# A two-layer hybrid decoder on one core: the same instructions with their SBUF buffers at other addresses

## The chip, the cores and the metric

The kernel runs on one core of one Trainium2 chip. The metric is device microseconds (us) for one execution of the whole program. Its engines are TensorE (PE for the matmuls, PEld for the loads of their weights), VectorE (DVE), ScalarE (ACT), GpSimd (POOL) and SyncE (SP), which issues the transfers from memory.

## The reference

Two layers act on x of 256 x 1024 float32. Cut to what matters here:

```
h = rms_norm(x, g_mix);  z = h @ w_in                 # 1024 -> 6072 columns
o_a, o_b, o_c = mla(z...), conv31(z...), nsa(z...)    # three mixers, each -> 1024
x = x + (g_a*o_a + g_b*o_b + g_c*o_c) @ w_out         # g = sigmoid of 3072 of z's columns
h = rms_norm(x, g_ffn)
x = x + square(relu(h @ w_ff1)) @ w_ff2               # 1024 -> 4096 -> 1024
```

## The kernel before

The large products are made in float32 precision from pieces that TensorE takes at full rate: each operand is split into a rounded high part and the remainder, hi + lo, and each product is three matmuls (hi·hi, hi·lo, lo·hi) into one PSUM bank. `piece` (lines 141 to 155) brings 128 x 1024 floats of a weight matrix into `raw` by one transfer, ACT rounds them into `hi` (line 153) and DVE writes the rest into `lo` (line 154).

There are two forms of product:

- `gemm_b` (lines 159 to 165) is channel-major. The weights are the stationary operand (128 columns, loaded anew for each matmul), and the activations stream past as 256 columns. The input projection (tile `psB` of `take`), the mixers' own projections (`wo` of `w_o`) and the first feed-forward product (`ff1`, shown as `ff`) have this form. A piece feeds 24 matmuls: 8 blocks k (or two times 4 in `w_o`), three each. Over both layers that are 1776 matmuls for `psB`, 576 for `wo`, and 1536 for `ff`.
- `gemm_a` (lines 167 to 173) is token-major. The activations are stationary, and the weights stream past as 512 columns. The second feed-forward product (`f0` to `f3`, shown as `f`, 768 matmuls), the product with w_out (its tiles are named `wo0` to `wo3` and show as `wo` too, but with 512 columns and tile `mh`, 192 matmuls) and the first projections (`psA`, 192 with 512 columns and 96 with 312) have it.

In the feed-forward stage one group is two `ff1` pieces (48 matmuls of 256 columns) and then four weight halves of the second product (24 matmuls of 512 columns), 16 groups a layer. Order of work: a priority for each step is written by hand (TRACE, URGENCY); the order of each engine's instructions is fixed when the program is built.

Where buffers lie is set by the tile pools. A pool places its tags one behind another, and a tag's buffers (`bufs`) lie one row length apart, so a row length that is no multiple of 256 bytes moves each next buffer to another place modulo 256. `hi` and `lo` have four buffers each of 1040 floats (4160 bytes, 16 x 256 + 64), taken in rotation. The table has the start of each buffer in the built program, modulo 256 bytes.

| buffer | role | before | after |
|---|---|---|---|
| hh, hl, oh, ol, h2, l2, mh, ml (tags hh, hl) | activations; stream in `gemm_b`, stationary in `gemm_a` | 128 | 64 |
| hi, lo, four buffers each | weights; stationary in `gemm_b`, stream in `gemm_a` | 128, 192, 0, 64 | 128 |
| hi2, lo2 (tag big, shown as hi, lo too) | weights that stream in `psA`, `wo` and `f` | 192 | 64 |
| rh, rl (tag pa, six buffers) | activations of the second feed-forward product, stationary | 192, 0, 64, 128, 192, 0 | 64 |
| yh, yl (tags cv, s2) | activations of `wo` for the convolution | 224 or 192, 128 | 64, 64 |
| raw | weights as transferred | 128 | 128 |

Blocks within a buffer lie a multiple of 256 bytes apart (512 for a block of weights, 1024 for a block of activations), so they leave these places as they are. Below, the offset of a matmul is the place of the stationary operand that is loaded next less that of the operand that streams meanwhile, modulo 256. In `gemm_b` before, the offsets are 0, 64, 128 and 192, one for each buffer of `hi` and `lo`.

Of the kernel before, what the change touches and what calls it, by code (L numbers as in the profile page):

```python
# [8 lines left out]
F32 = mybir.dt.float32  # L9
R32 = mybir.dt.float32r  # L10
# [3 lines left out]
ALU = mybir.AluOpType  # L14
AX = mybir.AxisListType

P = 128
D = 1024
T = 256
# [66 lines left out]
def trunk_kernel(ctx: ExitStack, tc: tile.TileContext, A, out, depth=DEPTH):  # L86
# [3 lines left out]
    wp = ctx.enter_context(tc.tile_pool(name="wp", bufs=3))  # L90
    ap_ = ctx.enter_context(tc.tile_pool(name="ap", bufs=1))
    sp = ctx.enter_context(tc.tile_pool(name="sp", bufs=2))
# [5 lines left out]
    def stat(n, name, dt=F32):  # L98
        return sp.tile([P, n], dt, tag="st%d" % n, name=name, bufs=2 if n > 64 else 6)

    S2 = 6
    PA = 6
    RB = 5
    S1 = 5
    WB = 4
# [5 lines left out]
    stt = nc.vector.scalar_tensor_tensor  # L111
# [24 lines left out]
    def raw(src, n):  # L136
        r = wp.tile([P, 1024], F32, tag="raw", name="raw", bufs=RB)[:, :n]
        nc.sync.dma_start(out=r, in_=src)
        return r

    def piece(src, k, ring=0, half=0):

        n = src.shape[-1]
        r = raw(src, n)
        if ring == 0:
            hi = wp.tile([P, 1040], R32, tag="hi", name="hi", bufs=WB)[:, :n]
            lo = wp.tile([P, 1040], R32, tag="lo", name="lo", bufs=WB)[:, :n]
        else:
            if half == 0:
                ring2[0] = (ap_.tile([P, 2048], R32, tag="big", name="hi2", bufs=BIG),  # L150
                            ap_.tile([P, 2048], R32, tag="big", name="lo2", bufs=BIG))
            hi, lo = (t[:, half * 1024:half * 1024 + n] for t in ring2[0])
        act(hi, r, AF.Copy)  # L153
        tt(out=lo, in0=r, in1=hi.bitcast(F32), op=ALU.subtract)  # L154
        return tuple(t.rearrange("p (k n) -> p k n", k=k) for t in (hi, lo))
# [23 lines left out]
    def rsqrt(v, p, n, name):  # L179

        s = stat(n, name + "_s", I32)
        y = stat(n, name + "_y")
        h = stat(n, name + "_h")
        t = stat(n, name + "_t")
        s, y, h, t = s[:p], y[:p], h[:p], t[:p]
        ts(out=s, in0=v.bitcast(I32), scalar1=1, scalar2=None, op0=ALU.logical_shift_right)
        ts(out=h, in0=v, scalar1=-0.5, scalar2=None, op0=ALU.mult)
        ts(out=y.bitcast(I32), in0=s, scalar1=-1, scalar2=0x5f3759df, op0=ALU.mult, op1=ALU.add)
        for _ in range(3):
            if n == 1:  # L190
                ts(out=t, in0=y, scalar1=y, scalar2=h, op0=ALU.mult, op1=ALU.mult)
                ts(out=y, in0=t, scalar1=1.5, scalar2=y, op0=ALU.add, op1=ALU.mult)
            else:
                tt(out=t, in0=y, in1=y, op=ALU.mult)
                tt(out=t, in0=t, in1=h, op=ALU.mult)
                stt(out=y, in0=t, scalar=1.5, in1=y, op0=ALU.add, op1=ALU.mult)
        return y
# [11 lines left out]
                op0=ALU.mult, op1=ALU.subtract)  # L209

    scaled = [None]
    splits = [None, None]
    tail_priority = [0]

# [11 lines left out]

    def sumsq_row(b, name, v):

        q = sp.tile([P, D // 2], F32, tag="s2", bufs=S2, name=name + "_q")
        s = stat(2, name + "_ss")  # L230
        for i in range(2):
            act(q, x[:, b, i * 512:(i + 1) * 512], AF.Square, accum_out=s[:, i:i + 1])
        tt(out=v, in0=s[:, 0:1], in1=s[:, 1:2], op=ALU.add)
        ts(out=v, in0=v, scalar1=1.0 / D, scalar2=EPS, op0=ALU.mult, op1=ALU.add)
        return v
# [18 lines left out]
    def layer(l):  # L254
# [15 lines left out]
        def s1(name):  # L270
            return sp.tile([P, T], F32, tag="s1", bufs=S1, name=name)

        def pa(name, dt=F32):
            return sp.tile([P, 528], dt, tag="pa", bufs=PA, name=name)[:, :512]

        hB = lambda t: (lambda k: t[k] if isinstance(t, list) else t[:, k, :])
        hA = lambda t, b: (lambda k: t[:, k, b * P:(b + 1) * P])
        col = lambda ap: ap.rearrange("p (n o) -> p n o", o=1)


        hh = ap_.tile([P, 8, T], R32, tag="hh", name="hh", bufs=2)
        hl = ap_.tile([P, 8, T], R32, tag="hl", name="hl", bufs=2)
        grow = raw(bass.AP(tensor=A["gmix"].tensor, offset=A["gmix"].offset + l * D, ap=[[0, P], [1, D]]), D)
        vs = stat(2, "n1v")
        for b in range(NB):
            now = tc.cur_priority
            if l > 0 and b == 0:

                tc.cur_priority = tail_priority[0]
            normed(x[:, b], b, rsqrt(sumsq_row(b, "n1", vs[:, b:b + 1]), P, 1, "n1"), grow, hh, hl, "n1t")  # L290
            if b == 0:
                behind = (scaled[0], splits[0], splits[1])
            tc.cur_priority = now
# [27 lines left out]
        def part_a(i):  # L321

            return ([psum(t, "psA%d" % i) for t in (("at", "at"), ("po", "ch"), ("at", "at"))[i]],
                    [piece(A["wA%d" % i][l, kp], 2, ring=int(i == 1), half=kp % 2) for kp in range(4)])

        def add_a(i, pw, b, kps=range(4)):
            for kp in kps:
                wh, wl = pw[1][kp]
                gemm_a(pw[0][b][:, :A_COLS[i]], hA(hh, b), hA(hl, b), lambda k: wh[:, k, :], lambda k: wl[:, k, :],
                       [(k, kp * 2 + k) for k in range(2)], first=(kp == 0), last=(kp == 3))  # L330


        def take(*names):

            ps = psum("mm", "psB")
            res = []
            for m, nm in enumerate(names):
                wh, wl = piece(A["wB"][l, B_TILES.index(nm)], 8)
                o = ps[:, m * T:(m + 1) * T]
                gemm_b(o, lambda k: wh[:, k, :], lambda k: wl[:, k, :], hB(hh), hB(hl), [(k, k) for k in range(8)])  # L340
                res.append((nm, o))
            return res, ps


        kr = ap_.tile([P, NB, 32], F32, tag="kr", name="kr")
        sg = ap_.tile([P, NB, 24], F32, tag="sg", name="sg")
        vsw = ap_.tile([P, NB, 2, P], F32, tag="vsw", name="vsw")
# [42 lines left out]
        def a_queries():  # L390
            nonlocal nr
            pw = part_a(2)
            psA = pw[0]
            for kp in range(4):
                for b in range(NB):
                    add_a(2, pw, b, (kp,))
            if l == 0:
                sp.tile([P, 8], F32, tag="gap2", name="gap2", bufs=1)
            for b in range(NB):
                pq = psA[b].rearrange("p (g j d) -> p g j d", g=2, j=4)  # L400
                sq = pa("nsqq").rearrange("p (n d) -> p n d", d=DH)
                qn.append(pa("qn").rearrange("p (n d) -> p n d", d=DH))
                act(sq.rearrange("p (j g) d -> p g j d", g=2), pq, AF.Square)
                act(qn[b].rearrange("p (j g) d -> p g j d", g=2), pq, AF.Copy)
                nc.vector.tensor_reduce(out=nst[:, b, 0:8], in_=sq, axis=AX.X, op=ALU.add)
            nv = stat(24, "nv")
            ts(out=nv, in0=nst.rearrange("p b n -> p (b n)"), scalar1=1.0 / DH, scalar2=EPS, op0=ALU.mult, op1=ALU.add)
            nr = rsqrt(nv, P, 24, "nr").rearrange("p (b n) -> p b n", b=NB)
# [330 lines left out]
                heads_T(xk, i, b, kTm, K("vk"), True)  # L739


        upad = sp.tile([P, 4, T + 30], F32, tag="cv", name="upad", bufs=2)
        ca = sp.tile([P, 4, T], F32, tag="cv", name="ca", bufs=2)

        def glu(i):
            if i == 0:
                nc.gpsimd.memset(upad[:, :, 0:30], 0.0)
            res, _ = take(("ua", i), ("ug", i))
            a_, g_ = s1("ua"), s1("ug")
            act(a_, res[0][1], AF.Identity, scale=0.5, bias=hv[:, i:i + 1])  # L750
            act(g_, res[1][1], AF.Tanh, scale=0.5, bias=hv[:, 4 + i:5 + i])  # L751
            stt(out=upad[:, i, 30:], in0=g_, scalar=1.0, in1=a_, op0=ALU.add, op1=ALU.mult)

        def taps(k0, k1):
            for k in range(k0, k1):
# [51 lines left out]
        def w_o(wn, th_, tl_, ko, c2):  # L807
            wh, wl = piece(A[wn][l, c2], 4)
            ps = psum("mm", "wo")
            for u in range(2):  # L810
                gemm_b(ps[:, u * T:(u + 1) * T], lambda k: wh[:, k, u * P:(u + 1) * P],
                       lambda k: wl[:, k, u * P:(u + 1) * P], hB(th_), hB(tl_), [(k, k + ko) for k in range(4)])
            return ps
# [85 lines left out]
        for b in range(NB):  # L899
            v = sumsq_row(b, "n2", stat(1, "n2_v"))  # L900
            rv = stat(1, "rv")
            nc.vector.reciprocal(rv, v)
            r2.append(rv)
# [23 lines left out]
    for l in range(depth):  # L927
        layer(l)
# [129 lines left out]
```

## Time and profile before

| | |
|---|---|
| three timed runs | 923.03, 923.93 and 928.15 us, median 923.93 |
| the profiled execution | 923.36 us, of which its instructions span 921.3 us |
| PE busy | 899.2 us, 98% of the span |
| DVE, ACT, POOL busy | 642.1, 537.3, 27.1 us |
| read from memory | 149.45 MB, 163 GB/s over the span |

[...] The duration does not tell how fast they follow each other; the difference between the starts of two matmuls, divided by the number of steps between them, does. It is called the pace below. The timeline shows starts to 10 ns, so over a run of 24 (23 steps) a pace is known to about half a nanosecond.

### The profile page before, as it was taken

To read this page: it belongs to the slowest core of one execution; us is meant where nothing else is said; L and a number is where in the kernel's file an instruction comes from. 1 tells how busy PE (TensorE), PEld (TensorE's weight loads), DVE (VectorE), ACT (ScalarE), POOL (GpSimd) and SP (SyncE) were. 2 spreads that over 40 slices of the span, in tenths; PEclk is the share of its full clock that TensorE was granted. 3 is DMA by queue.
4 is the path that set the end of the run, shared out by engine and by line. 5 is a ranking of instruction groups with operands and counts; after the bars stand their busy time and mean duration, and the time that the engine had idled before them with its cause. 6 is when DMAs were issued, how large, how long until landed. Compare 5 with 4: busy or idle time off the path is not lost.

```text
span 921.3 us, 16102 instructions
## 1 busy us (share of the span) xinstructions
PE 899.2 (98%) x6214; PEld 796.1 (86%) x6214; DVE 642.1 (70%) x1431; ACT 537.3 (58%) x987; POOL 27.1 (3%) x80
## 2 busy tenths in 40 slices
PE   5999999999999999999999999999999999999998
PEld 4899887699988999999878989877999889999996
DVE  6599988865787565555576989979558785555552
ACT  5456576987466554444355575779865575444430
POOL 3210000000000000000001000000000000000000
PEclk9999999999999999999999999999999999999999
DMA  8644622344556665665345563225436476555621
GB/s 286 219 164 147 218 87 80 115 134 140 181 188 204 210 203 185 190 194 186 102 160 188 165 217 104 79 80 183 155 97 199 151 262 211 185 191 193 188 92 46
DMA packets 43133, 151.55 MB, mean 164 GB/s; under 512 B 4784, under 2 KB 5680, under 8 KB 43056
## 3 DMA queue, kind: packets, MB, share of 16 engines
q1 hardware_dynamic: 43056, 150.52, 49.7%
q8 instruction: 49, 0.80, 0.4%
q14 instruction: 28, 0.23, 0.1%
HBM read 149.45 MB, written 1.05 MB: 163 GB/s over the span
## 4 chain that ended last, share of the span: by engine, by line
PE 89%; DVE 5%; DMA 3%; ACT 3%; issue 1%; SPq 0%; DVEq 0%; ACTq 0%
PE psB L163 7%; PE psB L165 7%; PE psB L164 7%; PE f L173 6%; PE f L171 6%; PE f L172 6%; PE ff L163 6%; PE ff L164 6%; PE ff L165 6%; PE wo L163 3%; PE wo L164 3%; PE wo L165 2%; DVE lo L154 2%; PE nS L578 2%; PE psA L172 2%; PE psA L173 2%
## 5 line engine op out<-in xcount | busy, mean ns | idle before, releaser
L154 DVE TENSOR_TENSOR lo<-raw,hi 128x1024 fp32r<-128x1024 f32 (+1 forms) x266 | 317.7, 1209 | 170.6 <-ACT hi L153 135.8
L153 ACT ACTIVATE hi<-raw 128x1024 fp32r<-128x1024 f32 (+1 forms) x266 | 274.2, 1048 | 256.1 <-DMA raw<-in_ff_dram 108.4
L163 PE MATMUL psB<-hh,hi 128*128 128x256 f32 x592 | 171.4, 290 | 1.5 <-ACT ug L751 1.4
L165 PE MATMUL psB<-hh,lo 128*128 128x256 f32 x592 | 169.1, 287 | 0.0
L164 PE MATMUL psB<-hl,hi 128*128 128x256 f32 x592 | 168.4, 285 | 0.0
L163 PE MATMUL ff<-h,hi 128*128 128x256 f32 x512 | 143.2, 281 | 0.0
L165 PE MATMUL ff<-h,lo 128*128 128x256 f32 x512 | 143.1, 280 | 0.0
L164 PE MATMUL ff<-l,hi 128*128 128x256 f32 x512 | 143.0, 280 | 0.0
L163 PEld LDWEIGHTS psB<-hh,hi 128*128 128x128 f32 x592 | 111.8, 189 | 8.3 <-issue 4.4
L165 PEld LDWEIGHTS psB<-hh,lo 128*128 128x128 f32 x592 | 111.5, 189 | 3.0 <-issue 2.6
L164 PEld LDWEIGHTS psB<-hl,hi 128*128 128x128 f32 x592 | 111.8, 189 | 0.3
L760 DVE SCALAR_TENSOR_TENSOR ca<-upad,cols,ca 128x256 f32<-128x256 f32 x240 | 103.7, 478 | 0.3
L173 PE MATMUL f<-hi,rl 128*128 128x512 f32 x256 | 101.1, 395 | 1.4 <-DVE rl L894 1.4
L171 PE MATMUL f<-hi,rh 128*128 128x512 f32 x256 | 100.9, 394 | 1.2 <-ACT rh L892 1.1
L172 PE MATMUL f<-lo,rh 128*128 128x512 f32 x256 | 100.6, 393 | 0.0
L163 PEld LDWEIGHTS ff<-h,hi 128*128 128x128 f32 x512 | 96.7, 189 | 1.2
L164 PEld LDWEIGHTS ff<-l,hi 128*128 128x128 f32 x512 | 96.5, 189 | 1.3
L165 PEld LDWEIGHTS ff<-h,lo 128*128 128x128 f32 x512 | 96.5, 189 | 0.0
L173 PEld LDWEIGHTS f<-hi,rl 128*128 128x128 f32 x256 | 48.0, 188 | 13.6 <-DVE rl L894 2.6
L171 PEld LDWEIGHTS f<-hi,rh 128*128 128x128 f32 x256 | 48.2, 188 | 11.2 <-ACT rh L892 1.6
L172 PEld LDWEIGHTS f<-lo,rh 128*128 128x128 f32 x256 | 48.1, 188 | 9.9
L172 PE MATMUL psA<-lo,hh 128*128 128x512 f32 (+1 forms) x96 | 36.4, 379 | 1.3 <-DVE lo L154 1.3
(279 smaller groups left out, 1420.2 us busy)
## 6 DMA issues: line engine op xcount, KB each, us to landing
raw<-in_ff_dram SPq DMA_DIRECT2D x128, 512.0 KB, 4.1
raw<-in_wB_dram SPq DMA_DIRECT2D x74, 512.0 KB, 4.0
raw<-in_wA_dram SPq DMA_DIRECT2D x16, 512.0 KB, 4.4
raw<-in_w_out_dram SPq DMA_DIRECT2D x16, 512.0 KB, 3.4
raw<-in_wo_nsa_dram SPq DMA_DIRECT2D x8, 512.0 KB, 4.9
raw<-in_wo_mla_dram SPq DMA_DIRECT2D x8, 512.0 KB, 3.8
raw<-in_wconv_dram SPq DMA_DIRECT2D x8, 512.0 KB, 3.5
raw<-in_wA_dram SPq DMA_DIRECT2D x8, 312.0 KB, 5.2
```

Source lines behind the costliest of these rows:

```text
L153: act(hi, r, AF.Copy)
L154: tt(out=lo, in0=r, in1=hi.bitcast(F32), op=ALU.subtract)
L163: mm(ps, lhsT=wh(kw), rhs=ah(ka), start=(first and i == 0), stop=False)
L164: mm(ps, lhsT=wh(kw), rhs=al(ka), start=False, stop=False)
L165: mm(ps, lhsT=wl(kw), rhs=ah(ka), start=False, stop=(last and i == n - 1))
L171: mm(ps, lhsT=ah(ka), rhs=wh(kw), start=(first and i == 0), stop=False)
L172: mm(ps, lhsT=ah(ka), rhs=wl(kw), start=False, stop=False)
L173: mm(ps, lhsT=al(ka), rhs=wh(kw), start=False, stop=(last and i == n - 1))
L578: mm(pS[g].rearrange("p (h z k) -> p h z k", h=nj, z=2)[:, i], lhsT=qTn[gs, 2 * jp + j, b * P:(b + 1) * P], rhs=kTn[gs, :, 0:nk], start=Tr ...
L760: stt(out=ca[:, i], in0=upad[:, i, k:k + T], scalar=K("wdw", 31 * i + k), in1=ca[:, i], op0=ALU.mult, op1=ALU.add)
```

## The change

The change alters row lengths and adds tiles that nothing uses (`gap0`, `gap1`, `gap3`, `gap4`, and a longer `gap2`). `hi` and `lo` get rows of 1024 floats instead of 1040, the tag `pa` 512 instead of 528, and the convolution's padded input 288 columns instead of 286, of which the last two are not used. No instruction is added, removed or moved: on each engine the built program has the same operations on the same tiles in the same order before and after, apart from the numbers of buffers and lines. Only addresses differ, as in the table: in all `gemm_b` products the offset becomes 64, and in the second feed-forward product the streaming and the stationary operand are at the same place (offset 0), except for its last group in each layer, whose weights are in `hi` and `lo` and stream at offset 192.

```diff
-            hi = wp.tile([P, 1040], R32, tag="hi", name="hi", bufs=WB)[:, :n]
-            lo = wp.tile([P, 1040], R32, tag="lo", name="lo", bufs=WB)[:, :n]
+            hi = wp.tile([P, 1024], R32, tag="hi", name="hi", bufs=WB)[:, :n]
+            lo = wp.tile([P, 1024], R32, tag="lo", name="lo", bufs=WB)[:, :n]
...
+        if name == "n1" and not gapped:
+            gapped.append(sp.tile([P, 16], F32, tag="gap4", name="gap4", bufs=1))
...
-            return sp.tile([P, 528], dt, tag="pa", bufs=PA, name=name)[:, :512]
+            return sp.tile([P, 512], dt, tag="pa", bufs=PA, name=name)
...
+        if l == 0:
+            ap_.tile([P, 48], F32, tag="gap0", name="gap0")
         hh = ap_.tile([P, 8, T], R32, tag="hh", name="hh", bufs=2)
...
+        if l == 0:
+            ap_.tile([P, 48], F32, tag="gap1", name="gap1")
         kr = ap_.tile([P, NB, 32], F32, tag="kr", name="kr")
...
-                sp.tile([P, 8], F32, tag="gap2", name="gap2", bufs=1)
+                sp.tile([P, 64], F32, tag="gap2", name="gap2", bufs=1)
...
-        upad = sp.tile([P, 4, T + 30], F32, tag="cv", name="upad", bufs=2)
+        if l == 0:
+            sp.tile([P, 40], F32, tag="gap3", name="gap3", bufs=1)
+        upad = sp.tile([P, 4, T + 32], F32, tag="cv", name="upad", bufs=2)
```

## Rows read from the trace of the kernel before

**Rows 1.** The page's part 1 and 2: engines and the granted clock

```profile
PE 899.2 (98%) x6214; PEld 796.1 (86%) x6214; DVE 642.1 (70%) x1431; ACT 537.3 (58%) x987; POOL 27.1 (3%) x80
...
PEclk9999999999999999999999999999999999999999
```

**Rows 2.** The page's part 4: the chain that ended last, by engine

```profile
PE 89%; DVE 5%; DMA 3%; ACT 3%; issue 1%; SPq 0%; DVEq 0%; ACTq 0%
```

**Rows 3.** The page's part 5: matmul groups, count, busy us, mean ns

```profile
L163 PE MATMUL psB<-hh,hi 128*128 128x256 f32 x592 | 171.4, 290 | 1.5 <-ACT ug L751 1.4
L163 PE MATMUL ff<-h,hi 128*128 128x256 f32 x512 | 143.2, 281 | 0.0
L173 PE MATMUL f<-hi,rl 128*128 128x512 f32 x256 | 101.1, 395 | 1.4 <-DVE rl L894 1.4
```

**Rows 4.** Timeline of PE, first feed-forward product: start us, us, line, tiles

```profile
336.69 0.28 PE L163 MATMUL ff<-h,hi 128*128 128x256 f32 x1
...
339.30 0.28 PE L165 MATMUL ff<-h,lo 128*128 128x256 f32 x1
...
347.90 0.28 PE L163 MATMUL ff<-h,hi 128*128 128x256 f32 x1
...
350.63 0.28 PE L165 MATMUL ff<-h,lo 128*128 128x256 f32 x1
350.75 0.28 PE L163 MATMUL ff<-h,hi 128*128 128x256 f32 x1
...
353.46 0.28 PE L165 MATMUL ff<-h,lo 128*128 128x256 f32 x1
...
361.85 0.28 PE L163 MATMUL ff<-h,hi 128*128 128x256 f32 x1
...
364.61 0.28 PE L165 MATMUL ff<-h,lo 128*128 128x256 f32 x1
...
443.15 0.28 PE L163 MATMUL ff<-h,hi 128*128 128x256 f32 x1
...
445.86 0.28 PE L165 MATMUL ff<-h,lo 128*128 128x256 f32 x1
```

**Rows 5.** Timeline of PE, products psB: one run of 24

```profile
206.82 0.28 PE L163 MATMUL psB<-hh,hi 128*128 128x256 f32 x1
...
209.53 0.28 PE L165 MATMUL psB<-hh,lo 128*128 128x256 f32 x1
```

**Rows 6.** Timeline of PE, second feed-forward product: where three stretches begin or end

```profile
331.16 0.39 PE L171 MATMUL f<-hi,rh 128*128 128x512 f32 x1
...
342.29 0.40 PE L171 MATMUL f<-hi,rh 128*128 128x512 f32 x1
...
353.58 0.39 PE L171 MATMUL f<-hi,rh 128*128 128x512 f32 x1
...
359.12 0.28 PE L163 MATMUL ff<-h,hi 128*128 128x256 f32 x1
```

**Rows 7.** Timeline of PE, 512-column products psA and wo

```profile
43.20 0.39 PE L173 MATMUL psA<-hi,hl 128*128 128x512 f32 x1
...
45.49 0.28 PE L163 MATMUL psB<-hh,hi 128*128 128x256 f32 x1
...
713.99 0.40 PE L171 MATMUL wo<-hi,mh 128*128 128x512 f32 x1
...
715.38 0.39 PE L171 MATMUL wo<-hi,mh 128*128 128x512 f32 x1
```

**Rows 8.** Windows: us, busy us and instructions of PE, PEld, DVE, ACT, POOL

```profile
60.00:90.00 30.00, 29.27 (x238) 27.71 (x237) 29.93 (x65) 19.62 (x41) 0.00 (x0) 1.00 0.47 150
...
285.00:470.00 185.00, 183.11 (x1173) 165.10 (x1173) 107.80 (x129) 89.84 (x119) 0.00 (x0) 1.00 0.57 181
```

**Rows 9.** The page's part 5: the splitting group of DVE

```profile
L154 DVE TENSOR_TENSOR lo<-raw,hi 128x1024 fp32r<-128x1024 f32 (+1 forms) x266 | 317.7, 1209 | 170.6 <-ACT hi L153 135.8
```

More of the change, by code (lines that the diff above doesn't have):

```diff
@@ L211, in trunk_kernel @@
     scaled = [None]
+    gapped = []
     splits = [None, None]
@@ L751, in glu @@
             act(g_, res[1][1], AF.Tanh, scale=0.5, bias=hv[:, 4 + i:5 + i])
-            stt(out=upad[:, i, 30:], in0=g_, scalar=1.0, in1=a_, op0=ALU.add, op1=ALU.mult)
+            stt(out=upad[:, i, 30:T + 30], in0=g_, scalar=1.0, in1=a_, op0=ALU.add, op1=ALU.mult)
         def taps(k0, k1):
```

## The prediction

> **What bounds the kernel now.** I read the page from the top. [...] The groups of part 5 then show what PE does: `psB`, `ff` and `f`, nearly without idle time before them [rows 3]. So the time is the number of matmuls times the pace at which they follow each other, and the group's mean durations (281, 290 and 395 ns) can't tell that pace, because matmuls overlap. I took it from the timeline, as the distance of starts.
>
> In the first feed-forward product each of the four weight buffers has a pace of its own [rows 4]. The runs of 24 (23 steps) take, by offset:
>
> - offset 0: 364.61 - 361.85 = 2.76 us, 120.0 ns a matmul;
> - offset 128: 350.63 - 347.90 = 2.73 us, 118.7 ns;
> - offset 192: 353.46 - 350.75 = 2.71 us, 117.8 ns;
> - offset 64: 339.30 - 336.69 = 2.61 us, 113.5 ns, but 445.86 - 443.15 = 2.71 us, 117.8 ns, in another run.
>
> [...] Offset 64 has two paces, and a run that is at one keeps it for all its 24 matmuls. Of the 15 unbroken runs of 24 at offset 64 in this product (the first is at 314.21, the last at 897.71 us; two stand in [rows 4]) 11 have the fast pace and 4 the slow one, a mean of 114.6 ns. The instructions and tiles are the same in all of these runs; the buffer is what differs. Pace and place go together in `psB` too, where one run at offset 64 takes 209.53 - 206.82 = 2.71 us, the slow pace [rows 5]; there some two fifths of the matmuls at offset 64 have the fast pace, since small products break its runs and each new start settles anew: a mean of 0.4 x 113.5 + 0.6 x 117.8 = 116.1 ns.
>
> **The change part by part.** All instructions stay, so each term is a number of matmuls by a difference of paces.
>
> First feed-forward product, 1536 matmuls [rows 3]: the four offsets hold a quarter each, (120.0 + 118.7 + 117.8 + 114.6) / 4 = 117.8 ns. After, all are at offset 64, 114.6 ns if the two paces share the runs as now. 3.2 ns x 1536 = 4.9 us less.
>
> `psB`, 1776 matmuls [rows 3], of which some 1460 follow their neighbour without a break: (120.0 + 118.7 + 117.8 + 116.1) / 4 = 118.2 now, 116.1 after, 2.1 x 1460 = 3.1 us less.
>
> `wo` of the mixers, 576 matmuls, three quarters of the way of `ff`, as their runs are mostly unbroken: 3.0 x 560 = 1.7 us less.
>
> `f`, 768 matmuls of 512 columns. Three stretches of 24 take 336.69 - 331.16 = 5.53, 347.90 - 342.29 = 5.61 and 359.12 - 353.58 = 5.54 us [rows 4, 6], which is 230.4, 233.8 and 230.8 ns, a mean of 231.7. They go to offset 0, where no matmul of `f` lies with both neighbours now. The nearest rows are six in a row of the w_out product at offset 0: 715.38 - 713.99 = 1.39 us, 231.7 ns [rows 7]. That is the mean of today, so I take the row and a change of 0.0; the best pace of any 512-column run here is that of ten `psA` matmuls at offset 192, 45.49 - 43.20 = 2.29 us, 229.0 ns [rows 7], and the worst the middle stretch above. The bounds are 2.1 us less and 1.6 us more. I put 0.4 us on the slow side, because in the 256-column product offset 0 is the slowest place.
>
> The other PE work (`psA`, w_out, transposes, attention) also gets new places: `psA` and w_out lose an offset of 192 in part and get one of 0 in part, between 229.0 and 231.7 ns on 384 matmuls, at most 1.0 us either way; I take 0.
>
> DVE and ACT: their operands move too. The 258 full splits of DVE have a mean of 1.22 us in each of the four buffers, with no more than 3 ns between them (their group is [rows 9]), so I cost their new places at nothing. What they hide behind is PE; between 60 and 90 us, DVE is busy for 29.93 of 30 us [rows 8], and the same stretch of the second layer is like it. There PE can't win: some 430 `psB` matmuls by 2.1 ns are 0.9 us that I give back. In the feed-forward stage DVE has 107.80 of 185 us and ACT 89.84 [rows 8], which is room enough for a PE that is 3% faster.
>
> Sum: -4.9 - 3.1 - 1.7 + 0.4 + 0.9 = -8.4 us. The profiled execution took 923.36 us, of which 2.1 lie around the span; it comes to 915.0. That execution is 0.6 us under the median of the timed runs, 923.93; I predict **915.3 us**.
>
> [...]
>
> **The rivals.**
>
> All runs settle at the fast pace. For it: nothing between the pieces changes the offset any more, and a run keeps its pace; after `f`, five of the six starts at offset 64 in the first layer went to the fast one (the run at 336.69 [rows 4] is one). Against it: in `psB` the breaks stay. The price: 4.3 x 1536 + 4.7 x 1460 + 4.3 x 560 = 15.9 us, less 2.0 for DVE's stretches, 923.4 - 13.9 = 909.5 us.
>
> No change. Either the place of a buffer as such, not its offset to the activations, sets the pace (each offset of `ff` now belongs to one buffer, so the rows can't tell these apart), or all runs settle at 117.8 ns, today's mean. Against the first: both layers and both products have the same paces by offset, while in the second layer the buffers come in another order. Either gives 923 us.
>
> DVE sets the end in the whole mixing stage, so that only `ff` and `wo` gain: -4.9 - 1.7 + 0.4 = -6.2, 917.2 us. Against it: PE is busy for 29.27 of 30 us even in DVE's fullest stretch [rows 8].
>
> Slower: in `f` the stream and the weights start at the same place in every matmul, with no matmul at another offset between to bring them apart. A 256-column matmul pays 6.5 ns more at offset 0 than at its best. If one of 512 columns pays that for each half, 13 ns, then `f` loses 768 x 13 = 10.0 us and the sum is 925.4 us; it is slower than before from 11 ns a matmul on (8.8 / 768), and by over 0.5% from 17 ns. The six matmuls of [rows 7] speak against it: they stand 2.7 ns above the best pace, not 13.
>
> **How the numbers follow.** The forecast has a chance of 0.50, the fast pace everywhere 0.22, no change 0.16, DVE's bound 0.08, slower 0.04. The forecast's own range is 911 to 919.5: the share of fast runs can be a half or nine tenths, and `f` can be at either bound. To hold 8 of 10 the range takes in most of the fast case and ends short of no change: 908.5 to 921.5. With 0.5% (4.6 us, about what a measurement tells from no change), faster is below 919.3: the fast case, most of the forecast and of DVE's bound, 0.78. Within 0.5% are no change and the rest of these, 0.19, slower 0.03.
>
> **What would show it.** In the profile after, unbroken runs of 24 `ff` and `psB` matmuls should take 2.61 or 2.71 us and none 2.76; if 2.73 and 2.76 are still there, the offset is not the cause. Six matmuls of `f` should take 1.37 to 1.40 us; 1.46 would be the slow rival. The share of the chain on DVE should rise above 5% if DVE's stretches take the gain. Wrong would be a faster kernel with unchanged paces, or better paces with PE's idle time grown by the same amount.

## The result and the profile after

The changed kernel takes 917.9 us (median of 6 runs, 915.4 to 920.0); the kernel before, run beside it, takes 923.5 (6 runs, 922.7 to 928.2). The ratio is 0.9934, 95% interval 0.9914 to 0.9954. By that ratio it is 6.1 us less (4.2 to 7.9); 915.3 us, and 8.6 less, was predicted. Run again later it took 917.5 (6 runs), ratio 0.992 (0.9896 to 0.9943). The total lies in the predicted range, but partly by luck: terms of the sum are wrong by some 3 us each in opposite directions, and cancel.

The page of the kernel after, the rows that answer to [rows 1, 2]: the engines with busy time, share and instructions, the granted clock in 40 slices, the chain that ended last.

```profile
PE 894.6 (98%) x6214; PEld 794.0 (87%) x6214; DVE 641.4 (70%) x1431; ACT 538.0 (59%) x987; POOL 27.1 (3%) x80
...
PEclk9999899999999999999999999999999999999999
...
PE 85%; DVE 7%; ACT 3%; DMA 3%; issue 2%; SPq 0%; DVEq 0%; ACTq 0%
```

PE has 4.6 us less, and DVE, ACT and the instruction counts are as before: nothing else became faster. One digit of the clock row is 8. The windows there (us, busy us and instructions of PE, PEld, DVE, ACT, POOL, then the granted clock, DMA share and GB/s) show it as 6.8 us at a granted clock of 0.50, with 1.00 on both sides:

```profile
85.00:90.00 5.00, 5.00 (x39) 4.23 (x37) 5.00 (x7) 3.38 (x7) 0.00 (x0) 1.00 0.46 125
90.50:97.30 6.80, 6.80 (x31) 6.52 (x31) 3.43 (x24) 2.87 (x10) 0.00 (x0) 0.50 0.95 342
100.00:105.00 5.00, 4.73 (x61) 3.89 (x60) 4.93 (x15) 4.41 (x9) 0.00 (x0) 1.00 0.16 35
```

PE is busy all through it. Six matmuls of `psB` in a row there:

```profile
93.20 0.41 PE L163 MATMUL psB<-hh,hi 128*128 128x256 f32 x1
...
94.27 0.41 PE L165 MATMUL psB<-hh,lo 128*128 128x256 f32 x1
```

1.07 us for five steps, 213.2 ns each with the trace's full digits, where the settled matmuls of `psB` in this profile have a mean of 115.2. By these two paces the stretch's work would take 3.7 us at 1.00, so some 3.1 us of the profiled 919.29 belong to the lower clock (an estimate). It comes without the change too: timed runs of the kernel before have mean clocks of 0.994 to 1.000 too, for instance 923.7 and 922.3 us at 1.000 and 928.2 and 926.8 at 0.994. The profile before happened to be a run without such a stretch, this one has one. Without it the profiled gain would be some 7.2 us, not 4.1.

The matmul groups of `ff` and `f` after (line, tiles, count, busy us, mean ns), for [rows 3]:

```profile
L163 PE MATMUL ff<-h,hi 128*128 128x256 f32 x512 | 143.5, 281 | 0.0
L173 PE MATMUL f<-hi,rl 128*128 128x512 f32 x256 | 100.1, 391 | 1.4 <-DVE n_v L237 0.7
```

`ff` has not moved (281 ns); `f` has (395 to 391). That the pieces `hi` and `lo` go at full rate is seen here only against the kernel's own plain float32 products. Two in a row before, of 512 columns:

```profile
178.16 0.59 PE L640 MATMUL uv<-raw,cq 128*128 128x512 f32 x1
...
178.59 0.59 PE L640 MATMUL uv<-raw,cq 128*128 128x512 f32 x1
```

They start 0.43 us apart, those of `f` 0.23 [rows 4, 6]. The timeline of PE after, one run of `ff`, the stretch of `f` behind it and the next run, for [rows 4, 6]:

```profile
325.95 0.28 PE L163 MATMUL ff<-h,hi 128*128 128x256 f32 x1
...
331.49 0.28 PE L165 MATMUL ff<-h,lo 128*128 128x256 f32 x1
331.61 0.40 PE L171 MATMUL f<-hi,rh 128*128 128x512 f32 x1
...
332.99 0.39 PE L171 MATMUL f<-hi,rh 128*128 128x512 f32 x1
...
337.07 0.28 PE L163 MATMUL ff<-h,hi 128*128 128x256 f32 x1
...
342.61 0.28 PE L165 MATMUL ff<-h,lo 128*128 128x256 f32 x1
```

Runs of `ff` are now 48 matmuls at one offset, 64. Both take 5.54 us for 47 steps, 117.8 ns: the slow of the two paces of offset 64. So do all 24 runs of 48 in both layers, and the two of 96 that follow `f` as well. In `f` the first six matmuls take 332.99 - 331.61 = 1.38 us, 230 ns each (231.2 with the trace's full digits), and the other 18 take 337.07 - 332.99 = 4.08 us, 226.7 ns. In the profile before, the best 17 steps in a row in `f` have 229.8 ns.

Adding up all distances from one start to the next by product gives PE's time in each (worked out from the whole timelines). "Repeat" is a second profile of the changed kernel, "cut" the version below with every entry cut. The profile before has no stretch at a granted clock of 0.50, after has the 6.8 us above, and repeat and cut have 3.4 us each:

| us | before | after | repeat | cut |
|---|---|---|---|---|
| `ff` | 182.5 | 181.5 | 180.7 | 175.6 |
| `psB` | 228.2 | 227.1 | 225.8 | 225.9 |
| `f` | 180.0 | 177.7 | 177.2 | 177.9 |
| `wo`, 256 columns | 70.0 | 68.1 | 69.1 | 70.0 |

### The profile page after: what moved, and what is told of

It is laid out like the page before. It is cut to its first block, busy times and chain, and to the rows that moved or that the text cites. A ratio compares the mean times of both kernels' runs of the same rounds, so it can differ in the third digit from the quotient of the medians.

```text
span 917.4 us, 16102 instructions
## 1 busy us (share of the span) xinstructions
PE 894.6 (98%) x6214; PEld 794.0 (87%) x6214; DVE 641.4 (70%) x1431; ACT 538.0 (59%) x987; POOL 27.1 (3%) x80
## 4 chain that ended last, share of the span: by engine, by line
PE 85%; DVE 7%; ACT 3%; DMA 3%; issue 2%; SPq 0%; DVEq 0%; ACTq 0%
PE psB L163 7%; PE psB L165 7%; PE psB L164 6%; PE f L173 6%; PE f L171 6%; PE f L172 6%; PE ff L165 6%; PE ff L164 6%; PE ff L163 6%; DVE lo L154 3%; PE nS L587 2%; PE wo L163 2%; PE wo L164 2%; PE wo L165 2%; PE psA L172 2%; ACT hi L153 2%
```

## Experiments

The theory after the result: the offset sets which paces a matmul stream can take, offset 64 can take two, and the entry into a run chooses between them. The first four kernels ran on one chip beside 29 runs of the kernel before (924.1 us).

**The weights alone.** Rows of 1024 floats in `hi` and `lo`, as in the change; the tag `pa` stays as before, so `f` keeps its mixed offsets. `gap2` to `gap4` and the padded input of the convolution are as before too. Against the changed kernel, the rest:

```diff
-            return sp.tile([P, 512], dt, tag="pa", bufs=PA, name=name)
+            return sp.tile([P, 528], dt, tag="pa", bufs=PA, name=name)[:, :512]
...
-            ap_.tile([P, 48], F32, tag="gap1", name="gap1")
+            ap_.tile([P, 16], F32, tag="gap1", name="gap1")
```

> Only the weights and activations of the channel-major products move: their offset is 64 (wo of the convolution apart); the second feed-forward product keeps the mixed places of before (its streaming weights at 192, its stationary ones at 192, 0, 64, 128). Theory (two paces at offset 64, and the stretch of f ahead of an ff run decides which): f stays at a mean of 231 ns as before; ff runs of 48 divide into runs at 113.3 and at 117.8 ns by the places of the f ahead, most of them fast as 5 of 6 were in the first layer before, so ff gains 4 to 6 us, psB and wo 3 us: 914 to 917 us. Rival (the gain of the change comes from f alone, offset 64 gives nothing): 922 to 924 us.

Measured: 920.7 us (12 runs), ratio 0.996 (0.9939 to 0.9982). `f` is unchanged at 231.2 ns (231.1 before). The timeline of PE, two neighbouring runs of `ff` at offset 64:

```profile
302.95 0.28 PE L163 MATMUL ff<-h,hi 128*128 128x256 f32 x1
...
308.48 0.28 PE L165 MATMUL ff<-h,lo 128*128 128x256 f32 x1
...
314.16 0.28 PE L163 MATMUL ff<-h,hi 128*128 128x256 f32 x1
...
319.49 0.28 PE L165 MATMUL ff<-h,lo 128*128 128x256 f32 x1
```

The first takes 5.53 us (117.7 ns), the second 5.33 (113.5). In layer 0, 8 of the 13 runs after `f` are fast, in a repeating pattern (slow, fast, slow, then two fast and one slow by turns); in layer 1 none is. So the 26 runs after `f` do gain here, 158.2 to 156.5 us (`ff` as a whole 182.5 to 179.3), and moving `f` as well takes this away: 158.3 in the changed kernel. The kernel is slower than the 914 to 917 us expected. Some 2 us of that are the slow runs of layer 1 (11 of 13, by 0.2 us each, had they been as often fast as expected), some 0.9 are `psB` and `wo`, which gained 2.1 us together instead of 3. The rest is not traced.

**The second product alone.** `pa` with rows of 512 and `hi`, `lo` as before. Against the kernel before:

```diff
-            return sp.tile([P, 528], dt, tag="pa", bufs=PA, name=name)[:, :512]
+            return sp.tile([P, 512], dt, tag="pa", bufs=PA, name=name)
...
+            ap_.tile([P, 32], F32, tag="gap1", name="gap1")
```

> Only the second feed-forward product moves to offset 0; the four buffers of the channel-major weights keep offsets 0, 64, 128, 192. Theory: f goes from 231.2 to 227 to 229 ns on 768 matmuls, 2 to 3 us less; ff keeps 120.0, 113.3 or 117.8, 118.7 and 117.8 ns by buffer: 920.5 to 921.5 us. Rival (f gains only where the run ahead is at offset 64): f stays at 231 ns, 923 to 924 us.

Measured: 923.6 us (12 runs), ratio 0.9993 (0.9977 to 1.001); the 920.5 to 921.5 expected was missed. `f` does gain (180.0 to 177.8 us), but the timeline shows `ff` behind it at offsets 64 and 128:

```profile
336.56 0.28 PE L163 MATMUL ff<-h,hi 128*128 128x256 f32 x1
...
339.27 0.28 PE L165 MATMUL ff<-h,lo 128*128 128x256 f32 x1
...
347.74 0.28 PE L163 MATMUL ff<-h,hi 128*128 128x256 f32 x1
...
350.50 0.28 PE L165 MATMUL ff<-h,lo 128*128 128x256 f32 x1
```

2.71 and 2.76 us, 118 and 120 ns, where the same runs took 2.61 and 2.73 before [rows 4]. All seven offset-64 runs of layer 0 are slow (in layer 1 all are fast), and all fourteen at offset 128 are at 119.8. Moving `f` changes the pace of its neighbour, whose addresses stay. The 26 runs of `ff` after `f` give back 0.7 us by it (158.2 to 158.9). The edit also moves more than `f`: the buffers `hi2` and `lo2` feed `psA` and the w_out product too, whose offset there becomes 64 instead of 192, and they go from 229.9 to 233.0 and from 230.3 to 232.9 ns, some 0.5 us on 192 matmuls. That leaves about 1 us of gain, which the interval (2.1 us less to 0.9 more) holds.

**Offset 0 with the buffers where the change puts them.** The activations move by 64 bytes instead of the weights.

```diff
-            ap_.tile([P, 48], F32, tag="gap0", name="gap0")
+            ap_.tile([P, 64], F32, tag="gap0", name="gap0")
...
-            ap_.tile([P, 48], F32, tag="gap1", name="gap1")
+            ap_.tile([P, 32], F32, tag="gap1", name="gap1")
```

> The changed kernel with its activations 64 bytes further on, so that hi and lo stay where the change put them, and the offset of all channel-major products is 0; f keeps offset 0. Theory (the offset sets the pace): ff, psB and wo run at 120.0 ns, 2.2 ns more than the mean of before on 1536, 1.8 on 1460, 2.2 on 560 matmuls, which is 7.2 us more than before, less 2.3 for f: 926 to 929 us. Rival (the place of the buffer itself sets the pace): as the changed kernel, 916 to 919 us.

Measured: 926.2 us (10 runs), ratio 1.0025 (1.0004 to 1.0046). A run of 48 `ff` matmuls:

```profile
303.18 0.28 PE L163 MATMUL ff<-h,hi 128*128 128x256 f32 x1
...
308.81 0.28 PE L165 MATMUL ff<-h,lo 128*128 128x256 f32 x1
```

5.63 us, 119.8 ns, and so are all others after `f`. The weights lie in the same places as in the changed kernel, so the place of the weights as such is out. The place of the activations as such is out too: in the kernel before they are all at 128, and the paces differ by the weights' place.

The expectation puts all channel-major products at offset 0, which leaves out one: the convolution's `wo` streams from `yh` and `yl`, which stay at 64 here, so it keeps offset 64. It serves as a control. Its 96 matmuls of layer 0 follow others of `wo` at offset 0 in the same execution; from the third to the last they read:

```profile
250.12 0.28 PE L165 MATMUL wo<-yh,lo 128*128 128x256 f32 x1
...
260.66 0.28 PE L165 MATMUL wo<-yh,lo 128*128 128x256 f32 x1
```

That is 10.54 us for 93 steps, 113.3 ns, while the other `wo` matmuls have a mean of 119.7. The weights lie at the same place and the kernel is the same: the offset is what differs.

**Other entries.** The changed kernel with the last `f` matmul ahead of a run cut in two, at another column for each group, and in three groups the first `ff` matmul instead.

```diff
-            mm(ps, lhsT=al(ka), rhs=wh(kw), start=False, stop=(last and i == n - 1))
+            if cut:
+                mm(ps[:, :cut], lhsT=al(ka), rhs=wh(kw)[:, :cut], start=False, stop=False)
+                mm(ps[:, cut:], lhsT=al(ka), rhs=wh(kw)[:, cut:], start=False, stop=(last and i == n - 1))
...
```

> The changed kernel, in which the last f matmul before nine of the ff runs of each layer is cut into two (256+256, 128+384, 384+128, 240+272, 272+240, 224+288, 288+224, 192+320, 320+192 columns), and the first ff matmul of three other runs into two (128+128, 64+192, 192+64). Theory (a run keeps the pace at which it starts, and the start is set by the phase in which f leaves the two streams): the 48 matmuls behind a cut are at 117.8 ns for some cuts and at 113.3 for others, the same in both layers; runs without a cut ahead stay at 117.8 as in the changed kernel. Rival (the feed-forward stage has one pace, set by its places): 117.8 ns behind every cut.

Measured: 915.1 us in one run. The timeline, the cuts 256+256 and 272+240 with the run behind each:

```profile
310.67 0.28 PE L180 MATMUL f<-hi,rl 128*128 128x256 f32 x1
310.79 0.28 PE L181 MATMUL f<-hi,rl 128*128 128x256 f32 x1
310.91 0.28 PE L169 MATMUL ff<-h,hi 128*128 128x256 f32 x1
...
316.44 0.28 PE L171 MATMUL ff<-h,lo 128*128 128x256 f32 x1
...
354.71 0.28 PE L180 MATMUL f<-hi,rl 128*128 128x272 f32 x1
354.83 0.28 PE L181 MATMUL f<-hi,rl 128*128 128x240 f32 x1
354.94 0.28 PE L169 MATMUL ff<-h,hi 128*128 128x256 f32 x1
...
360.28 0.28 PE L171 MATMUL ff<-h,lo 128*128 128x256 f32 x1
```

5.53 against 5.34 us, 117.8 against 113.6 ns, from one matmul ahead. Uncut, 256+256 and 192+320 leave the run slow; 128+384, 384+128, 240+272, 272+240, 224+288, 288+224, 320+192 and the three cuts of the first `ff` matmul make it fast, in both layers alike. A run that turns fast is there after some six matmuls. All sums, operands and addresses are the same. The entry chooses, and with 272+240 the cut and its run are shortest together; the two pieces take 233 ns where the uncut matmul takes 226, 7 more.

This run also bears on why `psB` is mixed. Up to its first cut, in `ff`, it does what the changed kernel does; yet the same 96 `psB` matmuls, started after a wait for ACT, take 10.88 us in it and 11.29 in the profile of the changed kernel:

```profile
74.96 0.39 PE L169 MATMUL psB<-hh,hi 128*128 128x256 f32 x1 [0.69 <-ACT ug L772]
...
85.84 0.28 PE L171 MATMUL psB<-hh,lo 128*128 128x256 f32 x1
```

```profile
75.72 0.39 PE L163 MATMUL psB<-hh,hi 128*128 128x256 f32 x1 [0.70 <-ACT ug L762]
...
87.01 0.28 PE L165 MATMUL psB<-hh,lo 128*128 128x256 f32 x1
```

In these profiles a run entered from the same work of PE gets the same pace each time (the 26 runs in both profiles of the changed kernel, each cut in both layers); this one, entered from a wait, got both. The 192 `wo` matmuls behind a `psB` run take over its pace: 21.65 us in the changed kernel's layer 0, 22.50 in the version with every entry cut, where nothing of `wo` is changed.

The next four ran on another chip, beside 11 runs of the kernel before (924.1 us).

**The changed kernel again**, as the control for the next.

> The changed kernel as it is, beside the next kernels on the same chip. All theories: ratio to the kernel before 0.991 to 0.996, some 918 us; the ff runs of 48 matmuls after f at 117.8 ns (5.54 us from the first start to the last), f at 227 ns.

Measured: 917.5 us (6 runs), ratio 0.992 (0.9896 to 0.9943). All 24 runs of 48 after `f` and both of 96 are at 117.8 ns once more.

**Every entry cut.** With the code of the kernel of other entries, the entry 272+240 ahead of all 26 runs, and no other edit.

```diff
+CUT_A = {g: 272 for g in range(13)}
```

> The changed kernel with the last f matmul before each ff run cut into 272 and 240 columns, in both layers: 26 matmuls more, the same sums. Theory (the pace of a run is set at its entry and then kept): all 26 ff runs after f go at 113.3 to 113.8 ns, 48 in 5.34 us instead of 5.54; that is 658 steps by 4.4 ns in each of two layers, -5.8 us, and 26 cuts by some 7 ns give back 0.2: some 5.6 us less than the changed kernel, 911.5 to 913.5 us, ratio to the kernel before about 0.987. Rival (what TensorE saves there, VectorE or a fall of the granted clock takes back): the same paces in the trace, and 916 to 918 us. Rival (it was chance that those runs were fast in the look before): ff runs at 117.8, no gain on the changed kernel.

Measured: 912.0 us (5 runs, 909.5 to 913.4), ratio 0.9858 (0.9832 to 0.9884): 5.5 us less than the control and 12 less than the kernel before, as expected (the trace's sum for `ff` is 5.1 less than the control's). The timeline, one of the 26 runs:

```profile
333.14 0.28 PE L169 MATMUL ff<-h,hi 128*128 128x256 f32 x1
...
338.48 0.28 PE L171 MATMUL ff<-h,lo 128*128 128x256 f32 x1
```

5.34 us in each of the 24 runs of 48. What PE saves comes off the end: no other engine took it back. This version beats both kernels.

**A cut in the middle.** The 25th matmul of a run cut, at nine columns; in layer 1 the entries cut as well. Against the version with every entry cut:

```diff
-CUT_B = {}
+CUT_B = {3: 128, 4: 64, 5: 192, 6: 144, 7: 112, 8: 32, 9: 224, 10: 240, 11: 16}
...
-                           cut=CUT_B.get(gi, 0) if u == 0 else 0)
+                           cut=CUT_B.get(gi, 0) if u == 1 else 0)
...
-                    acc_pass(po4, held[gi], rs[gi][0], rs[gi][1], 2 * NG, b, cut=CUT_A.get(gi, 0) if b == NB - 1 else 0)
+                    acc_pass(po4, held[gi], rs[gi][0], rs[gi][1], 2 * NG, b, cut=CUT_A.get(gi, 0) if b == NB - 1 and l == 1 else 0)
```

> The changed kernel with a cut in the middle: the 25th matmul of the ff run of groups 3 to 11 cut (128+128, 64+192, 192+64, 144+112, 112+144, 32+224, 224+32, 240+16, 16+240 in that order), in layer 1 with the cut of 272 and 240 columns ahead of each run besides. Theory (the pace is a state of the stream, kept until something breaks the rhythm): in layer 0 the first halves go at 117.8 and a part of the second halves at 113.3, from the cut on; in layer 1 the first halves go at 113.3 and some cuts may send the second half to 117.8. Rival (the pace goes with the entry from f, whose operands set it for the whole run): the second halves go on as the first began, whatever the cut.

Measured: 915.8 us in one run, at a granted clock of 1.00 throughout. The timeline: 64+192 in a run of layer 0 that began at 117.8 ns, then 112+144 in one of layer 1 that began at the fast pace:

```profile
322.91 0.28 PE L169 MATMUL ff<-h,hi 128*128 128x256 f32 x1
...
325.62 0.28 PE L171 MATMUL ff<-h,lo 128*128 128x256 f32 x1
325.74 0.20 PE L166 MATMUL ff<-h,hi 128*128 128x64 f32 x1
...
326.55 0.28 PE L169 MATMUL ff<-h,hi 128*128 128x256 f32 x1
...
328.48 0.28 PE L171 MATMUL ff<-h,lo 128*128 128x256 f32 x1
```

```profile
804.94 0.28 PE L169 MATMUL ff<-h,hi 128*128 128x256 f32 x1
...
807.56 0.28 PE L171 MATMUL ff<-h,lo 128*128 128x256 f32 x1
807.67 0.21 PE L166 MATMUL ff<-h,hi 128*128 128x112 f32 x1
...
808.13 0.28 PE L169 MATMUL ff<-h,hi 128*128 128x256 f32 x1
...
810.48 0.28 PE L171 MATMUL ff<-h,lo 128*128 128x256 f32 x1
```

The first goes from 2.71 / 23 = 117.8 ns to (328.48 - 326.55) / 17 = 113.5; the second from 113.9 to (810.48 - 808.13) / 20 = 117.5. Eight of nine cuts turn the pace from 117.8 to 113.5 ns in layer 0 (192+64 doesn't), one of nine turns it the other way in layer 1. So in this run the pace was the running stream's own: the same places and sums, and a break of the rhythm turned it either way, 117.8 to 113.5 and 113.9 to 117.5 ns.

**The cut without the change.** The kernel before with the entries 272+240, its four offsets as they were.

```diff
 # the kernel before, and
+CUT_A = {g: 272 for g in range(13)}
```

> The kernel before with the same cuts of 272 and 240 columns and nothing else, so with ff operands at offsets 0, 64, 128 and 192 by turns. Theory (offset 64 has two paces and the entry chooses; the other offsets have one): runs of 24 at offset 64 all at 113.3 (2.61 us), those at offset 0 still at 119.8, at 128 118.6, at 192 117.5; some 1 us less than before. Rival (the entry alone chooses, at any offset): all runs at about 113.3, 6 us less than before, and the moving of the buffers was not needed.

Measured: 922.4 us in one run; `ff` adds up to 182.0 us against 182.5. The timeline, a run at offset 64 and then one at 0, and one at 192 in layer 1:

```profile
336.56 0.28 PE L169 MATMUL ff<-h,hi 128*128 128x256 f32 x1
...
339.27 0.28 PE L171 MATMUL ff<-h,lo 128*128 128x256 f32 x1
339.39 0.28 PE L169 MATMUL ff<-h,hi 128*128 128x256 f32 x1
...
342.15 0.28 PE L171 MATMUL ff<-h,lo 128*128 128x256 f32 x1
...
810.25 0.28 PE L169 MATMUL ff<-h,hi 128*128 128x256 f32 x1
...
812.86 0.28 PE L171 MATMUL ff<-h,lo 128*128 128x256 f32 x1
```

2.71, 2.76 and 2.61 us. The rival falls: every run of 24 at offset 0 or 128 stays between 118.5 and 120.2 ns, so the moving of the buffers is needed. The theory as put is half wrong too: some offset-64 runs are slow behind the same cut, and two unbroken runs at 192 that follow the cut in layer 1 are fast. So 192 also has two paces, and the same cut does not help behind every stretch of `f` (here `f` has mixed offsets; that these make the difference is not shown).

## Why the prediction was right in sum and wrong in its terms

- **What bounds it** was right: PE is busy for 98% of the span before [rows 1] and after, its start-to-start distances are the time, and what the cut version took off `ff` (5.1 us against the repeat) came off the end (5.5).
- **The offset and not the place** is shown by the offset-0 kernel: with the weights where the changed kernel has them and the same instructions, `ff` goes at 119.8 ns instead of 117.8, and the convolution's `wo`, which keeps offset 64, at 113.3.
- **"Each of the four weight buffers has a pace of its own"** was too simple. In the trace of before, a run of 24 at offset 192 that starts at 894.99 us has 113.3 ns, against 117.6 to 117.9 in the other thirteen, and two of the fourteen at offset 128 have 119.9, against 118.4 to 118.8. Offset 64 was not the only one with two paces. The mean that the sum uses is hardly changed by it.
- **`ff`, -4.9 us: the step that failed.** It read "114.6 ns if the two paces share the runs as now". They don't: the share is not a property of the offset but of the entry, and the change altered the entry as well, by moving `f`. All 26 runs after `f` went slow: a mean of 117.8 ns over their steps, where the four offsets together had 117.7 before, so nothing by pace. The 1.0 to 1.8 us that the sums of `ff` still lost lie in the start of the stage and its first pieces. The half of the second rival that read "all runs settle at 117.8 ns" came true, for this product alone.
- **`f`, +0.4 us: mis-sized.** It measured -2.3 and -2.8 us, just past the lower bound of -2.1. The six matmuls of [rows 7] were read rightly (231.7 ns; the first six have 231.2 in 24 of the 26 stretches after) but they stand just behind a place with another offset; from the seventh on the pace is 226.7. No row of before showed a settled stretch at offset 0, and my bound from the nearest rows, 229.0, was 2 ns too high.
- **`psB`, -3.1, with 0.9 given back where DVE is full:** the first term had the right size. The settled pace (distances of 105 to 125 ns between neighbours) went from 117.9 to 115.2 and 114.8 ns, and the time fell by 3.2 us in the middle-cut run (225.0 us, at a granted clock of 1.00 throughout), with nothing to be given back from it. The 1.1 and 2.4 us of the two profiles above hold 4.3 and 2.8 us of `psB` at a granted clock of 0.50, of which a little under half is the price (an estimate from the 213.2 and 115.2 ns above). The 0.9 given back was wrong. "There PE can't win", the prediction says of 60 to 90 us; the same stretch of PE's work, from one matmul of `psB` to another, before and then after:

```profile
60.03 0.28 PE L164 MATMUL psB<-hl,hi 128*128 128x256 f32 x1
...
89.81 0.36 PE L163 MATMUL psB<-hh,hi 128*128 128x256 f32 x1
```

```profile
60.59 0.28 PE L164 MATMUL psB<-hl,hi 128*128 128x256 f32 x1
...
89.92 0.37 PE L163 MATMUL psB<-hh,hi 128*128 128x256 f32 x1
```

29.78 us became 29.33, and the stretch like it in the second layer (505 to 540 us) 34.84 became 34.16; the repeat has the same. PE gained 1.1 us where the prediction had nothing. By the paces there it would have been some 1.5; what took the rest is not traced. The sign named for it, DVE's share of the chain above 5%, came out at 7, 6 and 5% (after, repeat, cut), which tells nothing.
- **`wo`, -1.7:** -1.9, -0.9 and 0.0 in three profiles; the two runs of 192 are both fast in the first, one of each in the repeat and both slow in the cut version, 0.85 us apiece. That it came near -1.7 once is luck.
- **The slow rival**, `f` at offset 0 paying 13 ns more, is out; so is the fast rival, 909.5, for the uncut kernel. The price of its first term was right (6.6 us): with the entries cut `ff` goes from 182.5 to 175.6.
- **Slips in the working:** 923.93 - 8.4 is 915.5 and not 915.3, and the slow rival's 10.0 in place of the 0.4 makes 925.1 and not 925.4. Neither changes what follows.

The errors of `ff` (some 3 to 4 us too much gain) and of `f` (some 3 us too little) cancel, which is luck. In the repeat the four products of the table sum to -1.8 - 2.4 - 2.8 - 0.9 = -7.9 against the predicted -8.4, with other addends. Its profiled execution, with some 3.4 us at a granted clock of 0.50 in it, took 916.74 us, 6.6 less than before's.

What stays open: why one cut turns the stream and another doesn't; no row shows the state itself. That the uncut `f` at offset 0 led into the slow pace in all 26 runs of both profiles of the changed kernel is measured, not explained. That places count modulo 256 bytes is how the table is kept; no run tries another period.

## What to carry to other kernels

Where PE is busy throughout, read the distance of starts by runs and by the operands' addresses, not the mean duration: a few ns a matmul were 1.4% here. When a run has two paces, don't carry their shares over to a changed kernel: ask what the run is entered from, and measure the entry together with the run. A split of one matmul ahead of a long stream can be worth more to that stream than moving its buffers (5.1 us of `ff` here, against none by pace); ahead of the four offsets of the kernel before the same splits took 0.5 us off `ff`.

## What the runs showed of the hardware that was not expected

- A stream of 256-column matmuls at offset 64 goes on at 113.3 or at 117.8 ns for 192 matmuls without drifting (`wo` above); one cut matmul ahead, 7 ns dearer, turns the run behind it, at some columns of the cut and not at others. No run of 24 `ff` matmuls was below 119.5 ns at offset 0, and none below 118.4 at offset 128, in the profiles that have them.
- 512-column matmuls with both operands at one place settle at 226.7 ns after about six, while the mixed offsets of `f` stay at 231.
- The granted clock fell to 0.50 for 3 to 7 us in some executions, of the changed kernel at 90.5 us in one and near 122 us in the next, with DMA share at 0.95 in the first and 0.7 to 0.8 in the second. Runs of the kernel before with mean clocks of 0.994 to 1.000 spread over some 6 us, 922.3 to 928.2.
